# A conv block with an MLP on one core: where the sums of activations are staged, and after which products the gate columns come

## Chip, core, metric

One core of one Trainium2 chip. The metric is the device time of one execution in microseconds (us). The engines are TensorE (PE, with its weight loads PEld), VectorE (DVE), ScalarE (ACT), GpSimd (POOL) and SyncE (SP), whose queue issues nearly all DMAs, in order. Matmuls write to banks of PSUM, the other operands lie in SBUF.

## What is computed

One layer over 256 tokens of width 2048, in float32. For the kernel that is measured (`DEPTH` is 1) the mixer is the convolution.

```python
mod = silu(c) @ mod_w + mod_b                      # 2048 -> 6 x 2048
sh1, sc1, g1, sh2, sc2, g2 = split(mod, 6)
h = rms_norm(x, norm1_g) * (1 + sc1) + sh1
a, gt = split(h @ conv_w_in + conv_b_in, 2)
u = depthwise_conv(a * sigmoid(gt), width 31) + conv_dw_b
y = silu(layer_norm(u)) @ conv_w_out + conv_b_out
x = x + (1 + g1) * y
h = rms_norm(x, norm2_g) * (1 + sc2) + sh2
u = square(relu(h @ mlp_w1))                       # 2048 -> 8192
x = x + (1 + g2) * (u @ mlp_w2)                    # 8192 -> 2048
```

The change lies in the last two lines and in g2, the gate of the last one.

## The kernel before

**Precision by splitting.** Every float32 operand of a matmul is split into a rounded part `hi` (made by ACT, L228) and the remainder `lo` (a subtraction on DVE, L232; in earlier parts on POOL). A product is the sum of three matmuls, hi by hi, hi by lo, lo by hi. Weights arrive in tiles of 128 x 2048 (1024 KB) in a ring of seven `raw` buffers; each is split in two halves, into a ring of six `hi` and one of six `lo` buffers, 128 x 1024 each. ACT can fill a `hi` buffer only when its last reader is done.

**The MLP.** The hidden width is cut into four quarters. Of each quarter q come the "up" products (`mlp_w1`), then eight "down" products (`mlp_w2`), here called up 0, down 0, up 1 and so on. A down product i takes two weight tiles, so four halves, and issues 48 matmuls. Two down products fill one block of the output: even i starts it in a PSUM bank pair, odd i ends it (function `regions`; there are two such pairs, named `mm`). The order of the products is 0, 2, 1, 3, 4, 5, 6, 7. A finished block is emptied into the running output `y`, by ACT in down 0 (L1341), by an addition on DVE in down 1 and down 2 (L1343, "drain"), before its bank pair can be started again. In quarters 1 to 3 part of the up products is replaced by seven smaller ones, in the manner of Strassen ("seven"), four of which take sums and differences of the activations `hl` in place of `hl` itself.

**The sums.** These are the same for quarters 1 to 3. `make_sums(k2)` makes a quarter of them, four times in down 0: DVE adds hi and lo of two tiles (`a` and `b`, L353), takes four differences (`c` and `d`, L359), ACT rounds these (L363), DVE takes the remainder (L364), and eight DMAs write both to a DRAM buffer `kept` (L367), from which `load_sum` reads them at the start of each later up stage. `a`, `b`, `c`, `d` come from `two`, a ring of six buffers of 128 x 512 that many steps share. The rounded part and the remainder lie in a tile `st` from the ring of `hi` buffers. `SUMS_AT` lists the down products behind which a quarter of the sums is made.

**Gate columns.** The 16 tiles of g2 are each a product of a 128 x 2048 tile of `mod_w` with `silu(c)`, made by DVE as one long multiply with accumulation (L538, in `mod_col`) and a small addition (L493). Such a "column" takes one `raw` buffer and one load of 1024 KB. `LATE_GATE` tells after which up or down product how many of them are issued.

**Order.** A scheduler orders each engine's instructions from a priority, given by the place in the program, and its own time line. `urgent()` moves what stands in it ahead, as it does the splits of the next product's weights; `tc.issue_after(x)` keeps what stands in it behind instruction x on its engine. `state["w_lo"]` is the last weight remainder issued so far, `state["w_hi"]` the last rounding. DVE, ACT and SP carry out their instructions in that order.

Of the kernel before, what the change touches and what calls it, by code (L numbers as in the profile page):

```python
# [9 lines left out]
F32 = mybir.dt.float32  # L10
F32R = mybir.dt.float32r
AF = mybir.ActivationFunctionType
ALU = mybir.AluOpType
PSUM = bass.MemoryType.PSUM

P = 128
# [51 lines left out]
SPLIT_LOADS = [("col", SC1 * KT + KT - 1), ("col", SH1 * KT + KT - 1), ("first", KT - 1)]  # L68
POOLED = [("out", i) for i in range(6)] + [("up", 0, 1), ("up", 0, 2)]
IN_PSUM = range(1, 6)  # L70
LATE_GATE = {("up", 0): [0, 0, 0, 0, 1, 1, 1, 0], ("down", 0): [1, 1, 0, 0, 0, 0, 0, 0], ("down", 1): [0, 3, 0, 3, 3, 2, 0, 0]}
SEVEN = (1, 2, 3)
SUMS_AT = (2, 3, 4, 5)
SEVEN_JOBS = (1, 5, 7, (2,), 3, (3,), 6, (6,), 2, 4, (7,))
PLAIN = {"x": 4, "w": 0, "z": 1, "y": 5}
PLUS = {5: "w", 7: "z", 6: "z", 4: "y"}
# [3 lines left out]
def conv_block(ctx: ExitStack, tc: tile.TileContext, x, vec, dwq, c_row, mod_r, mod_t, mod_c, w_first, w_in, w_out, w1, w2, out):  # L80
    nc = tc.nc

    const = ctx.enter_context(tc.tile_pool(name="const", bufs=1))
    wts = ctx.enter_context(tc.tile_pool(name="wts", bufs=1))
# [38 lines left out]
    for i in range(2):  # L123
        p = ps.tile([P, 2, 2 * T], F32, name="mm", bufs=2)
# [6 lines left out]
    state = {"used": 0}  # L131
# [12 lines left out]
    def urgent():  # L144
        return tc.high_priority(offset=URGENT)

    HALF = KT // 2
# [202 lines left out]
    def make_sums(k2):  # L350
        a, b, c, d = [two() for _ in range(4)]
        for dst, src in ((a, hl[k2]), (b, hl[k2 + 4])):
            nc.vector.tensor_tensor(dst, src[:, :, 0:T].bitcast(F32), src[:, :, T : 2 * T].bitcast(F32), op=ALU.add)  # L353
        one, two_ = slice(0, P), slice(P, 2 * P)
        for dst, x0, x1 in (
            (c[:, :, one], a[:, :, two_], b[:, :, two_]), (d[:, :, one], a[:, :, one], c[:, :, one]),
            (c[:, :, two_], a[:, :, two_], a[:, :, one]), (d[:, :, two_], b[:, :, one], d[:, :, one]),
        ):
            nc.vector.tensor_tensor(dst, x0, x1, op=ALU.subtract)  # L359
        for ms, src in (((0, 2), c), ((1, 3), d)):  # L360
            st = wts.tile([P, HALF, P], F32R, name="hi", bufs=6).rearrange("p (h k m) n -> p h k m n", h=2, k=2)
            src = src.rearrange("p k (m n) -> p k m n", m=2)
            nc.scalar.activation(st[:, 0], src, AF.Copy)  # L363
            nc.vector.tensor_tensor(st[:, 1], src, st[:, 0].bitcast(F32), op=ALU.subtract)  # L364
            for j, m in enumerate(ms):
                for h in range(2):
                    nc.sync.dma_start(kept[m, :, 2 * k2 : 2 * k2 + 2, h, :], st[:, h, :, j, :].bitcast(F32))  # L367

    def load_sum(m):
        sums_of[m] = []  # L370
# [211 lines left out]
    def ps_two():  # L582
        return ps.tile([P, 2, T], F32, name="acc", bufs=2)

    def two():
        return tmp.tile([P, 2, T], F32, name="two", bufs=6)
# [6 lines left out]
    def spread(r):  # L593
        return r[:, None, :].to_broadcast([P, 2, T])
# [7 lines left out]
    def scaled(k2, r):  # L602
        n = two()
        nc.vector.tensor_tensor(n, pair_of(xs, k2), spread(r), op=ALU.mult)
        return n

    def modulate(k2, n, sh, sc, h):
        for c in range(2):
            k = 2 * k2 + c
            nc.scalar.activation(h[:, c, :], n[:, c, :], AF.Identity, scale=amps[sc][:, k : k + 1], bias=mcol(sh, k))  # L610
        split_act(new_hl(k2), h)
# [25 lines left out]
    for job in jobs:  # L637
        n = quota.get(job, 0)
# [3 lines left out]
        if job == ("in", KT - 2):  # L642
            after[job] = after[job] + scales
        if job[:2] in LATE_GATE:
            n = LATE_GATE[job[:2]][job[2]]
            after[job], last = last[:n], last[n:]
# [39 lines left out]
    def evac(p, cs=slice(0, 2), out=None):  # L686
        t1 = two()[:, cs, :]
        t2 = two()[:, cs, :] if out is None else out
        nc.scalar.activation(t1, p[:, cs, T : 2 * T], AF.Copy)
        nc.vector.tensor_tensor(t2, p[:, cs, 0:T], t1, op=ALU.add)  # L690
        return t2
# [3 lines left out]
    p = ps.tile([P, 512], F32, name="small", bufs=1)  # L695
    for k2 in range(HALF):
        s = two()
# [8 lines left out]
    with urgent():  # L706
        part = two()[:, 0, :]
        nc.scalar.activation(part, p[:, 0:T], AF.Copy)
        p = ps.tile([P, 512], F32, name="row", bufs=1)
# [8 lines left out]
    for _ in range(2):  # L718
        p = ps.tile([P, 2, 2 * T], F32, name="mm", bufs=2)
# [52 lines left out]
    for k in range(KT):  # L772
        c = k % 2
# [3 lines left out]
        if c == 0:  # L777
            n = two()
# [5 lines left out]
        h = h2[:, c, :]  # L784
# [121 lines left out]
    def fold_stats(sums):  # L906
        st = ps.tile([P, 2, 2 * T], F32, name="mm", bufs=2)
        for n in range(2):
            nc.tensor.matmul(st[:, n, 0:T], col("fold", n * P, P), sums, start=True, stop=False)
        return st  # L910
# [80 lines left out]
    def at_job(at, f, *args):  # L991
        tasks.setdefault(at, []).append(partial(f, *args))
# [40 lines left out]
    for n, job in enumerate(jobs):  # L1033
# [16 lines left out]
        kind, i = job[0], job[-1]  # L1050
# [14 lines left out]
        if kind == "out" and i > 0:  # L1065
            p = ps_two()
        elif not by_tokens(job):
            p = ps.tile([P, 2, 2 * T], F32, name="mm", bufs=2)
# [48 lines left out]
        if kind == "in":  # L1117
# [57 lines left out]
            with urgent(), tc.issue_after(state["row_end"].ins):  # L1175
                st = fold_stats(sums)
# [18 lines left out]
            with urgent():  # L1195
# [3 lines left out]
                ms = factor[:, T : 2 * T]  # L1199
# [4 lines left out]
            for k2 in range(HALF):  # L1204
# [17 lines left out]
                with urgent():  # L1222
                    nc.gpsimd.tensor_tensor(e, pair_of(cvs, k2), spread(mu), op=ALU.subtract)
                    state["e_end"] = nc.vector.tensor_tensor(e, e, spread(r), op=ALU.mult).ins
                    for c in range(2):
                        k = 2 * k2 + c
# [17 lines left out]
        if kind == "out":  # L1244
# [4 lines left out]
            with urgent():  # L1249
                for c in range(2):  # L1250
                    k = 2 * i + c
# [10 lines left out]
            a = two()  # L1262
            for c in range(2):
                k = 2 * i + c
# [27 lines left out]
        elif kind == "up":  # L1292
            if job[1:] == (0, 0):
                for k2 in range(HALF):
                    modulate(k2, scaled(k2, r2), SH2, SC2, ps_two())
            if plain:
                with urgent():
                    t2 = evac(p)
                    a = two()
                    nc.vector.tensor_tensor(t2, t2, spread(r2), op=ALU.mult)  # L1300
                    for c in range(2):
                        at = 2 * i + c
                        nc.scalar.activation(t2[:, c, :], t2[:, c, :], AF.Relu, bias=shc[:, at : at + 1])
                    nc.vector.tensor_tensor(a, t2, t2, op=ALU.mult)
                u2[i] = mp.tile([P, 2, 2 * T], F32R, name="u2", bufs=HALF)
                split_act(u2[i], a)
            elif i % 2 and job[1] in SEVEN:
                at_job(n + 1, block_out, n + 1, job[1], i // 2, sums.pop((kind, i // 2)))
            elif i % 2:
                with urgent():  # L1310
                    turn_block(job[1], i // 2, sums.pop((kind, i // 2)))
            mods(after[job])
            if job[1] == 0:
                if i == 0:
                    turned = scratch.tile([KT, P, T], F32, name="turned")
                    y = xs.rearrange("p k t -> p (k t)").rearrange("p (b f) -> p b f", b=2)
                turn(i)
        else:
            with tc.issue_after(state["w_lo"]):
                mods(after[job])  # L1320
            if job[1] == 0 and i in SUMS_AT:
                if i == SUMS_AT[0]:
                    kept = scratch.tile([4, P, HALF, 2, P], F32, name="kept")
                make_sums(SUMS_AT.index(i))
            if job == ("down", 1, 5):
                gates = scratch.tile([1, D], F32, name="gates")
                with tc.issue_after(state["load"].ins):
                    nc.sync.dma_start(gates[0].rearrange("(k p) -> p k", p=P), modc[:, G2 * KT : G2 * KT + KT])
            if job == ("down", 1, 7):
                with tc.issue_after(state["load"].ins):  # L1330
                    nc.sync.dma_start(cb, gates.to_broadcast([P, D]))
            if job[1] == 2 and i % 2 == 0:
                with tc.issue_after(state["load"].ins):
                    pieces[i // 2] = fetch(i // 2)
            if i % 2 == 0:
                continue
            for t, cs, p in sums.pop((kind, i // 2)):
                at = slice(512 * (i // 2) + cs.start, 512 * (i // 2) + cs.stop)
                s = y[:, t, at]
                if job[1] == 0:  # L1340
                    nc.scalar.activation(s, p, AF.Copy)  # L1341
                elif job[1] < QUARTERS - 1:
                    nc.vector.tensor_tensor(s, p, s, op=ALU.add)  # L1343
                    if job[1] == 2 and i < HALF - 1:
                        scale_y(s, at, pieces[i // 2][t])
                    elif job[1] == 2:
                        at_job(n + 4, scale_y, s, at, pieces[i // 2][t])
                else:
                    g = two().rearrange("p a t -> p (a t)")[:, cs]
                    with tc.issue_after(state["y_end"].ins) if "y_end" in state else ExitStack():  # L1350
                        nc.vector.tensor_tensor(g, p, cb[:, at], op=ALU.mult)
                    state["y_end"] = nc.vector.tensor_tensor(s, s, g, op=ALU.add)
                    nc.sync.dma_start(out[:, t, at], s)
# [60 lines left out]
```

## Time and profile before

| | |
|---|---|
| median of three runs | 1092.16 us (1090.88 to 1093.37) |
| the profiled execution | 1096.91 us, span 1095.1 us |
| PE busy | 1065.1 us, 97% of the span |
| DVE, ACT, POOL busy | 844.5, 582.2, 216.1 us |
| mean granted TensorE clock | 0.994 |
| DMA | 331.00 MB, 302 GB/s on average |

The profile is of one execution, which took 0.4% more than the median. A line such as L232 is the line of the kernel's source. `out<-in` names tiles; a releaser behind an arrow is what ended an idle time. PE is reported busy for nearly the whole span, and matmuls overlap, so a stage is better judged by how long its fixed number of matmuls takes.

### The profile page before, as it was taken

What the parts mean: (1) busy time and instruction counts of PE and PEld (TensorE: products, weight loads), DVE (VectorE), ACT (ScalarE), POOL (GpSimd) and SP (SyncE); (2) the same over time, 40 slices, a digit from 0 to 9 for tenths busy, and PEclk for the clock granted to TensorE, in tenths of its full rate; (3) what the DMA queues carried; (4) which work ended last, traced back from release to release, by engine and by line L of the source; (5) the groups of instructions that cost most, each with busy time, mean ns of one, the idle gap of its engine ahead of it and who ended that gap; (6) DMA issues with size and microseconds to landing.
All of it is one profiled execution on the core that took longest, in us unless ns stands there. A gap on an engine that the chain in (4) does not pass through costs nothing.

```text
span 1095.1 us, 15654 instructions
## 1 busy us (share of the span) xinstructions
PE 1065.1 (97%) x5928; PEld 880.1 (80%) x5928; DVE 844.5 (77%) x1105; ACT 582.2 (53%) x805; POOL 216.1 (20%) x147
## 2 busy tenths in 40 slices
PE   7999999999999999999999999699999999999998
PEld 4888876777799988887787888588888888788887
DVE  5777899988678878768478994888896678898563
ACT  4111398677875685444356475235565634556541
POOL 0000169989498270000000000000000000000000
PEclk9999999999999999999999999899999999999999
DMA  9999997997999868988775899985979983979921
GB/s 386 420 421 420 416 414 290 390 353 272 416 403 396 334 241 292 309 238 283 251 269 203 293 314 297 374 339 162 369 220 347 234 301 139 293 254 362 262 78 39
DMA packets 154478, 331.00 MB, mean 302 GB/s; under 512 B 88482, under 2 KB 114594, under 8 KB 119458
## 3 DMA queue, kind: packets, MB, share of 16 engines
q1 hardware_dynamic: 154256, 329.88, 83.3%
q8 instruction: 46, 0.75, 0.3%
q14 instruction: 30, 0.24, 0.1%
q10 hardware_dynamic: 146, 0.13, 0.0%
HBM read 313.71 MB, written 16.26 MB: 301 GB/s over the span
## 4 chain that ended last, share of the span: by engine, by line
PE 58%; DMA 19%; DVE 12%; SPq 4%; issue 3%; ACT 3%; DVEq 0%; ACTq 0%
DMA raw<-mod_c 10%; PE mm L297 9%; PE mm L298 9%; PE mm L299 9%; PE mm L260 6%; DVE lo L232 4%; DMA flat<-two 3%; SPq L404 3%; PE mm L261 3%; DVE raw L538 3%; PE acc L257 2%; PE acc L256 2%; PE acc L258 2%; DMA kept<-hi 2%; PE mm L950 2%
## 5 line engine op out<-in xcount | busy, mean ns | idle before, releaser
L228 ACT ACTIVATE hi<-raw 128x1024 fp32r<-128x1024 f32 x356 | 366.7, 1055 | 296.0 <-PE mm L299 180.6
L232 DVE TENSOR_TENSOR lo<-raw,hi 128x1024 fp32r<-128x1024 f32 x295 | 351.1, 1218 | 129.1 <-ACT hi L228 128.4
L297 PE MATMUL mm<-hi,u 128*128 128x512 f32 x496 | 194.5, 393 | 9.0 <-DVE x L1343 7.9
L298 PE MATMUL mm<-lo,u 128*128 128x512 f32 x496 | 194.8, 394 | 2.0 <-DVE lo L232 2.0
L299 PE MATMUL mm<-hi,u 128*128 128x512 f32 x496 | 194.1, 392 | 1.1 <-DVE u L246 1.1
L232 POOL TENSOR_TENSOR lo<-raw,hi 128x1024 fp32r<-128x1024 f32 x61 | 155.0, 2567 | 30.7 <-ACT hi L228 30.7
L538 DVE SCALAR_TENSOR_TENSOR raw<-raw,cond 128x2048 f32<-128x2048 f32 x50 | 116.0, 2332 | 30.8 <-DMA raw<-mod_c 30.8
L297 PEld LDWEIGHTS mm<-hi,u 128*128 128x128 f32 x496 | 94.1, 190 | 29.4 <-issue 8.2
L298 PEld LDWEIGHTS mm<-lo,u 128*128 128x128 f32 x496 | 94.2, 190 | 22.7 <-DVE lo L232 3.5
L299 PE MATMUL mm<-hi,hl 128*128 128x512 f32 x288 | 112.1, 389 | 0.0
L298 PE MATMUL mm<-lo,hl 128*128 128x512 f32 x288 | 112.0, 389 | 0.0
L297 PE MATMUL mm<-hi,hl 128*128 128x512 f32 x288 | 112.0, 389 | 0.0
L299 PEld LDWEIGHTS mm<-hi,u 128*128 128x128 f32 x496 | 94.2, 190 | 21.1 <-DVE u L246 1.5
L829 DVE SCALAR_TENSOR_TENSOR acc<-u,v,acc 128x256 f32<-128x256 f32 x230 | 91.5, 483 | 0.0
L260 PE MATMUL mm<-hl,hi 128*128 128x512 f32 x224 | 80.0, 401 | 0.0
L733 PE MATMUL mm<-two,first 128*128 128x256 f32 x240 | 57.5, 394 | 7.9 <-ACT two L791 7.9
L256 PE MATMUL acc<-hl,hi 128*128 128x256 f32 x224 | 63.4, 283 | 0.0
L257 PE MATMUL acc<-hl,hi 128*128 128x256 f32 x224 | 63.4, 283 | 0.0
L258 PE MATMUL acc<-hl,lo 128*128 128x256 f32 x224 | 63.4, 283 | 0.0
L298 PEld LDWEIGHTS mm<-lo,hl 128*128 128x128 f32 x288 | 54.1, 188 | 11.3
L297 PEld LDWEIGHTS mm<-hi,hl 128*128 128x128 f32 x288 | 54.1, 188 | 11.2
L299 PEld LDWEIGHTS mm<-hi,hl 128*128 128x128 f32 x288 | 54.1, 188 | 11.2
(265 smaller groups left out, 1681.2 us busy)
## 6 DMA issues: line engine op xcount, KB each, us to landing
raw<-w SPq DMA_DIRECT2D x128, 1024.0 KB, 7.3
raw<-mod_c SPq DMA_DIRECT2D x64, 1024.0 KB, 10.6
raw<-mod_r SPq DMA_DIRECT2D x28, 1024.0 KB, 8.5
raw<-w_in SPq DMA_DIRECT2D x16, 1024.0 KB, 10.5
raw<-w_out SPq DMA_DIRECT2D x16, 1024.0 KB, 8.6
first<-w_first SPq DMA_DIRECT2D x15, 1024.0 KB, 19.8
u<-kept SPq DMA_DIRECT2D x24, 512.0 KB, 7.6
flat<-two SPq DMA_DIRECT2D x30, 256.0 KB, 6.1
```

What stands on the lines that cost most here:

```text
L228: state["w_hi"] = nc.scalar.activation(hi, w[:, ks, :], AF.Copy).ins
L232: end = by.tensor_tensor(lo, w[:, ks, :], hi.bitcast(F32), op=ALU.subtract)
L256: nc.tensor.matmul(out_p, w, m[:, 0:T], start=begin, stop=False)
L257: nc.tensor.matmul(out_p, w, m[:, T : 2 * T], start=False, stop=False)
L258: state["mm_end"] = nc.tensor.matmul(out_p, lo[:, k % HALF, :], m[:, 0:T], start=False, stop=end)
L260: nc.tensor.matmul(p[:, c, :], hi[:, k % HALF, :], m, start=(k == 0), stop=(k == KT - 1))
L297: nc.tensor.matmul(p, p_hi, hi, start=begin, stop=False)
L298: nc.tensor.matmul(p, p_hi, lo, start=False, stop=False)
L299: nc.tensor.matmul(p, p_lo, hi, start=False, stop=end)
L538: end = nc.vector.scalar_tensor_tensor(w, w, 1.0, cb, op0=ALU.mult, op1=ALU.mult, accum_out=acc)
L733: step = nc.tensor.matmul(held[n][:, c, :], w[:, 2 * n + c, :], h, start=k == 0 and c == 0, stop=k == KT - 1, skip_group_check=True)
L829: end = nc.vector.scalar_tensor_tensor(out, s, w, acc, op0=ALU.mult, op1=ALU.add)
```

## The change

Three things change. The tiles `st` are gone: the rounded parts go into `a` and `b`, which are no longer needed then, and the remainders into `c` and `d` in place; the DMAs write from there. The sums are made behind products 2, 1, 3, 4 instead of 2, 3, 4, 5, and kept behind the last weight split. The gate columns are spread anew over the products, and kept behind the last drain on DVE that was issued before them.

```diff
-LATE_GATE = {("up", 0): [0, 0, 0, 0, 1, 1, 1, 0], ("down", 0): [1, 1, 0, 0, 0, 0, 0, 0], ("down", 1): [0, 3, 0, 3, 3, 2, 0, 0]}
+LATE_GATE = {("up", 0): [0, 0, 0, 1, 1, 1, 1, 0], ("down", 0): [1, 0, 0, 0, 0, 1, 1, 0], ("down", 1): [0, 2, 0, 2, 2, 3, 0, 0]}
-SUMS_AT = (2, 3, 4, 5)
+SUMS_AT = (2, 1, 3, 4)
...
-        for ms, src in (((0, 2), c), ((1, 3), d)):
-            st = wts.tile([P, HALF, P], F32R, name="hi", bufs=6).rearrange("p (h k m) n -> p h k m n", h=2, k=2)
-            src = src.rearrange("p k (m n) -> p k m n", m=2)
-            nc.scalar.activation(st[:, 0], src, AF.Copy)
-            nc.vector.tensor_tensor(st[:, 1], src, st[:, 0].bitcast(F32), op=ALU.subtract)
+        for ms, src, hi in (((0, 2), c, a), ((1, 3), d, b)):
+            nc.scalar.activation(hi.bitcast(F32R), src, AF.Copy)
+            nc.vector.tensor_tensor(src.bitcast(F32R), src, hi, op=ALU.subtract)
             for j, m in enumerate(ms):
-                for h in range(2):
-                    nc.sync.dma_start(kept[m, :, 2 * k2 : 2 * k2 + 2, h, :], st[:, h, :, j, :].bitcast(F32))
+                for h, part in enumerate((hi, src)):
+                    nc.sync.dma_start(kept[m, :, 2 * k2 : 2 * k2 + 2, h, :], part[:, :, P * j : P * j + P])
...
-            with tc.issue_after(state["w_lo"]):
+            with tc.issue_after(state["w_lo"]), tc.issue_after(state.get("drain", state["w_lo"])):
                 mods(after[job])
...
-                make_sums(SUMS_AT.index(i))
+                with tc.issue_after(state["w_lo"]):
+                    make_sums(SUMS_AT.index(i))
...
-                    nc.vector.tensor_tensor(s, p, s, op=ALU.add)
+                    state["drain"] = nc.vector.tensor_tensor(s, p, s, op=ALU.add).ins
```

From L360 on the changed kernel's lines are one or two lower: L364 is L362 there, L538 is L536, L1343 is L1342. PE's order is the same in both, and POOL's.

On DVE, in down 0, before, the second of the four sums and the start of the third. L353 to L364 are the sum, L232 the remainder of a weight half.

```order
L353 TENSOR_TENSOR two<-hl 128x512 x2
L232 TENSOR_TENSOR lo<-raw,hi 128x1024
L359 TENSOR_TENSOR two<-two 128x2x128
L364 TENSOR_TENSOR hi<-two,hi 128x512
L359 TENSOR_TENSOR two<-two 128x2x128
L364 TENSOR_TENSOR hi<-two,hi 128x512
L359 TENSOR_TENSOR two<-two 128x2x128
L353 TENSOR_TENSOR two<-hl 128x512 x2
L359 TENSOR_TENSOR two<-two 128x2x128 x3
L232 TENSOR_TENSOR lo<-raw,hi 128x1024
```

On DVE at the same place now, the first sum and the start of the second:

```order
L353 TENSOR_TENSOR two<-hl 128x512 x2
L359 TENSOR_TENSOR two<-two 128x2x128 x2
L232 TENSOR_TENSOR lo<-raw,hi 128x1024
L359 TENSOR_TENSOR two<-two 128x2x128 x2
L232 TENSOR_TENSOR lo<-raw,hi 128x1024
L362 TENSOR_TENSOR two<-two 128x512 x2
L232 TENSOR_TENSOR lo<-raw,hi 128x1024 x2
L353 TENSOR_TENSOR two<-hl 128x512 x2
L359 TENSOR_TENSOR two<-two 128x2x128 x2
```

Before, parts of successive sums ran into each other; now each sum is spread over the four weight halves of one product, and the next begins behind them.

On ACT, in down 0, before: L228 rounds a weight half, L363 the sums, L1341 empties a block, L243 rounds a hidden activation.

```order
L243 ACTIVATE u_4640<-two 128x2x256
L228 ACTIVATE hi<-raw 128x1024
L363 ACTIVATE hi<-two 128x512 x2
L228 ACTIVATE hi<-raw 128x1024 x6
L1341 ACTIVATE x_2504<-mm 128x512 x2
L228 ACTIVATE hi<-raw 128x1024 x2
```

On ACT at the same place now:

```order
L243 ACTIVATE u_4640<-two 128x2x256
L243 ACTIVATE u_4644<-two 128x2x256
L228 ACTIVATE hi<-raw 128x1024 x4
L361 ACTIVATE two<-two 128x512 x2
L228 ACTIVATE hi<-raw 128x1024 x4
L1340 ACTIVATE x_2504<-mm 128x512 x2
```

The roundings of a sum no longer write into the ring of `hi` buffers, and stand behind four weight halves each.

On DVE, in down 1, before, from the splits of the last two hidden activations (u_6093, u_6098, L246) to the additions that empty the first two blocks (L1343); L538 is a gate column, L493 its small addition.

```order
L246 TENSOR_TENSOR u_6093<-two,u_6093 128x2x256
L232 TENSOR_TENSOR lo<-raw,hi 128x1024
L538 SCALAR_TENSOR_TENSOR raw,modc<-raw,cond 128x2048 x3
L246 TENSOR_TENSOR u_6098<-two,u_6098 128x2x256
L232 TENSOR_TENSOR lo<-raw,hi 128x1024
L493 TENSOR_TENSOR modc<-modc,v 128x1 x2
L232 TENSOR_TENSOR lo<-raw,hi 128x1024 x2
L493 TENSOR_TENSOR modc<-modc,v 128x1
L232 TENSOR_TENSOR lo<-raw,hi 128x1024
L538 SCALAR_TENSOR_TENSOR raw,modc<-raw,cond 128x2048 x3
L1343 TENSOR_TENSOR x_2504<-mm,x_2504 128x512 x2
```

On DVE at the same place now:

```order
L246 TENSOR_TENSOR u_6093<-two,u_6093 128x2x256
L232 TENSOR_TENSOR lo<-raw,hi 128x1024
L536 SCALAR_TENSOR_TENSOR raw,modc<-raw,cond 128x2048 x2
L246 TENSOR_TENSOR u_6098<-two,u_6098 128x2x256
L232 TENSOR_TENSOR lo<-raw,hi 128x1024
L491 TENSOR_TENSOR modc<-modc,v 128x1 x2
L232 TENSOR_TENSOR lo<-raw,hi 128x1024 x3
L1342 TENSOR_TENSOR x_2504<-mm,x_2504 128x512 x2
L536 SCALAR_TENSOR_TENSOR raw,modc<-raw,cond 128x2048 x2
L232 TENSOR_TENSOR lo<-raw,hi 128x1024
L1342 TENSOR_TENSOR x_2504<-mm,x_2504 128x512 x2
```

Two columns instead of three stand ahead of the split of u_6098, and the next ones have moved from ahead of the first additions to behind them.

## The prediction

> **What bounds the kernel now.** I read the times first, then the page's share of engines, then the busy time by stage, and only then single rows. TensorE (PE) is busy nearly everywhere, so what can be won is where it is not. The MLP alternates "up" products (the first matrix) and "down" products (the second) by quarter of the hidden width. The view of windows, cut at the edges of those stages, has per row: the stretch and its length, busy time of PE, weight loads, DVE, ACT and POOL, the granted clock, the DMA share and GB/s.
>
> ```profile
> span 1095.1 us, 15654 instructions
> 474.60:567.90 93.30, 90.13 (x386) 72.86 (x385) 64.55 (x81) 40.84 (x50) 0.00 (x0) 0.98 0.84 280
> 567.90:651.90 84.00, 82.21 (x362) 67.43 (x361) 74.80 (x66) 53.59 (x61) 0.00 (x0) 1.00 0.71 243
> 651.90:751.10 99.20, 90.26 (x385) 73.83 (x384) 75.67 (x82) 40.12 (x44) 0.00 (x0) 0.95 0.90 320
> 751.10:833.10 82.00, 81.92 (x361) 67.51 (x360) 73.90 (x68) 51.99 (x58) 0.00 (x0) 1.00 0.82 282
> 833.10:920.20 87.10, 87.10 (x386) 72.12 (x385) 57.48 (x60) 40.11 (x44) 0.00 (x0) 1.00 0.86 270
> ```
>
> These are down 0, up 1, down 1, up 2 and down 2. The three down stages issue the same 384 matmuls (the view adds one or two at the edges). Down 2 takes 87.10 us with PE busy throughout, so 10.89 us for each of its eight products is the price without a stall. Against it down 0 loses 6.2 us and down 1 loses 12.1. Up 1 loses 2.0 against up 2, which does the same work. Together 20.3 us: the change touches nothing else that waits, and this is its ceiling.
>
> Where they are lost, from PE's timeline (start, duration, idle before and releaser):
>
> ```profile
> 511.16 0.50 PE L298 MATMUL mm<-lo,u 128*128 128x512 f32 x1 [0.76 <-DVE lo L232]
> 545.68 0.50 PE L297 MATMUL mm<-hi,u 128*128 128x512 f32 x1 [1.19 <-ACT hi L228]
> 546.94 0.79 PE L298 MATMUL mm<-lo,u 128*128 128x512 f32 x1 [0.76 <-DVE lo L232]
> 549.66 0.61 PE L298 MATMUL mm<-lo,u 128*128 128x512 f32 x1
> 550.09 0.42 PE L299 MATMUL mm<-hi,u 128*128 128x512 f32 x1
> 581.23 0.50 PE L347 MATMUL acc<-lo,u 128*128 128x512 f32 x1 [1.66 <-DVE lo L232]
> 692.09 0.50 PE L299 MATMUL mm<-hi,u 128*128 128x512 f32 x1 [1.09 <-DVE u L246]
> 696.53 0.39 PE L299 MATMUL mm<-hi,u 128*128 128x512 f32 x1
> 704.77 0.76 PE L297 MATMUL mm<-hi,u 128*128 128x512 f32 x1 [7.86 <-DVE x L1343]
> 705.34 0.63 PE L298 MATMUL mm<-lo,u 128*128 128x512 f32 x1
> 705.76 0.63 PE L299 MATMUL mm<-hi,u 128*128 128x512 f32 x1
> ```
>
> In down 0 PE waits for split weights, in down 1 above all for the addition of L1343, which empties a bank. Each longer wait is paid twice: behind it a matmul starts every 0.43 us (549.66 to 550.09, 705.34 to 705.76) instead of every 0.227 (87.10 by 384).
>
> **Sums through the `two` buffers.** ACT's timeline shows why the weights are late in down 0:
>
> ```profile
> 508.78 4.86 ACT L228 ACTIVATE hi<-raw 128x1024 fp32r<-128x1024 f32 x5 [8.36 <-DMA kept<-hi]
> 531.12 2.95 ACT L228 ACTIVATE hi<-raw 128x1024 fp32r<-128x1024 f32 x3 [7.90 <-DMA kept<-hi]
> 544.57 2.95 ACT L228 ACTIVATE hi<-raw 128x1024 fp32r<-128x1024 f32 x3 [8.50 <-DMA kept<-hi]
> 557.44 6.75 ACT L228 ACTIVATE hi<-raw 128x1024 fp32r<-128x1024 f32 x7 [6.97 <-DMA kept<-hi]
> ```
>
> Four sums each put two staging tiles into the ring of six `hi` buffers, so ACT's next split waits 7 to 8.5 us until the writes to `kept` have landed: 31.7 us of ACT, of which PE feels 6.2 and, through a DVE that enters up 1 late, the 1.66 at 581.23. The change takes these tiles away. Its work stays: per sum two additions from `hl`, four half-size differences, two roundings on ACT, two remainders and eight writes, with the same shapes. Nothing is saved in busy time, only the four waits. But the wait does not vanish. `two` has six buffers and a sum now uses four until its writes land; so the next sum finds two free for its additions, and its differences wait for the writes of the first two. That wait sits on DVE, and queued behind it are the `lo` splits that PE needs, and the roundings on ACT with the `hi` splits behind them. What it costs I work out from these rows:
>
> ```profile
> 474.62 0.39 PE L297 MATMUL mm<-hi,u 128*128 128x512 f32 x1
> 492.68 0.69 DVE L416 SCALAR_TENSOR_TENSOR two<-two 128x512 f32<-128x512 f32 x1 [0.53 <-DMA two<-flat]
> 481.96 1.27 DVE L353 TENSOR_TENSOR two<-hl 128x512 f32<-128x512 f32 x2
> 522.37 0.76 DVE L359 TENSOR_TENSOR two<-two 128x256 f32<-128x256 f32 x2
> 535.63 1.29 DVE L364 TENSOR_TENSOR hi<-two,hi 128x512 fp32r<-128x512 f32 x2
> 479.09 2.31 DVE L232 TENSOR_TENSOR lo<-raw,hi 128x1024 fp32r<-128x1024 f32 x2
> 522.18 7.58 SPq L367 DMA_DIRECT2D kept<-hi  x8
> L367 SPq DMA_DIRECT2D kept<-hi x32: 359/486/1437, 495.5 to 553.0; - x32
> DMA to landing us min/median/max: 3.0/6.6/8.6
> ```
>
> The first sum now starts behind the last square (492.68, released by a transfer, which the change does not move), one split, two splits of `u` (0.6 each) and two more: 493.4 + 1.1 + 1.2 + 2.3 = 498.0. It takes 1.2 for the additions, 0.7 and 0.7 for the differences, a split behind each (1.1), 1.2 for the remainders: 504.0. The writes start when the first remainder is done, 0.6 earlier, behind one weight load on SP's queue (0.35). By the medians the last one that counts is issued 7 x 0.49 later and lands 6.6 later: 9.8 after the sum's end. The next sum then needs the second pair of differences, a split and the remainders, 3.0. So a sum takes 12.8 us where a product takes 10.9, and DVE falls back 1.9 us a sum: ends at 504.0, 516.8, 529.6, 542.4. The last sum holds the splits of product 6, which PE wants at 474.62 + 6 x 10.89 = 540.0 and, the second, 2.7 later. They are done 4.0 and 1.2 before 542.4, at 538.4 and 541.2: 1.6 and 1.5 us to spare. Before, ACT and DVE were already late at 511.16. So I expect the waits of down 0 to go nearly whole and leave 0.7 for jitter: 6.2 - 0.7 = 5.5.
>
> Bounds: with landings at the minimum, 3.0, a sum takes 9.2 and nothing is left (6.2). At the maximum, 8.6, it takes 14.8; the last sum ends at 548.4 and its second split 4.5 us late, 6 with the half clock: nothing is won. I take the median because the eight writes follow 1024 KB weight loads now as then.
>
> In up 1 the DVE then starts earlier. Two columns have moved into products 5 and 6 (2.2 each) and eat part of it, so I count 1.4 of the 2.0.
>
> The sums at products 2, 1, 3, 4 instead of 2, 3, 4, 5 issue no more. The last writes land by 542.4 + 9.8 = 552, and the first product that reads `kept` is the second of up 1, some 5 us after 474.6 + 87.1 = 561.7: nothing waits for them. On SP's queue the writes stand ahead of weight loads, which wait for DVE's splits to empty a `raw` buffer; seven of these, three and a half products of weights, cover that.
>
> **Gate columns.** DVE's timeline in down 1:
>
> ```profile
> 684.72 2.28 DVE L538 SCALAR_TENSOR_TENSOR raw<-raw,cond 128x2048 f32<-128x2048 f32 x1
> 691.35 0.69 DVE L246 TENSOR_TENSOR u<-two,u 128x512 fp32r<-128x512 f32 x1
> 691.95 1.22 DVE L232 TENSOR_TENSOR lo<-raw,hi 128x1024 fp32r<-128x1024 f32 x1
> 696.71 2.29 DVE L538 SCALAR_TENSOR_TENSOR raw<-raw,cond 128x2048 f32<-128x2048 f32 x1
> 703.34 1.29 DVE L1343 TENSOR_TENSOR x<-mm,x 128x512 f32<-128x512 f32 x2
> ```
>
> Three columns (684.72 to 691.35, 2.21 each with their accumulator read) precede the last split of `u`; three more (696.71 to 703.34) precede the additions. Now two stand in front of that split: it starts at 684.72 + 4.42 = 689.1 and ends at 689.7, where PE issued its last matmul before the wait at 690.62 (692.09 less 1.09 idle and the 0.38 of the matmul before). Then four weight splits (4 x 1.14) and small additions (0.2) end at 694.5, and now come the additions of L1343, 0.60 each: first half of the bank at 695.1, second at 695.7. PE ends its fourth product at 651.9 + 4 x 10.89 = 695.4 and wants the second half three matmuls (0.7) later. So the two waits (1.36 and 10.8 with the half clock) go, with 0.3 us to spare; I leave 0.5. The columns follow the additions, two by two, 4.4 beside 4.6 of splits and 1.3 of additions in 10.9: they fit, product 5's three too (6.6 + 4.6 = 11.2, additions 1.2, by a DVE which then is over 5 us ahead). Gain 12.1 - 0.5 = 11.6, between 12.1 and 9 (a lateness of one column's half, 1.1, and its half clock, 2).
>
> The loads move with the columns: sixteen of 1024 KB as before, two less in down 1. In down 0 and in up 0 one more each. Of up 0:
>
> ```profile
> 411.07 1.21 DVE L232 TENSOR_TENSOR lo<-raw,hi 128x1024 fp32r<-128x1024 f32 x1
> 427.82 2.29 DVE L538 SCALAR_TENSOR_TENSOR raw<-raw,cond 128x2048 f32<-128x2048 f32 x1 [1.67 <-DMA raw<-mod_c]
> ```
>
> The new column stands ahead of the split at 411.07, whose product starts at 474.62 - 5 x 10.89 = 420.2: 8 us of cover against 2.2 plus a load's wait like the 1.67 here. Cost nothing; without the cover 4.
>
> **Sum.** 5.5 + 1.4 + 11.6 = 18.5 us of a span of 1095.1, whose execution took 1096.91. The median of three runs is 1092.16, 0.4% less, and the gain scales to 18.4: 1073.7.
>
> **Rivals.** First, the wait only changes engine: landings near 8.6 keep down 0 and up 1 as they are and only down 1 gains: 1092.2 - 11.6 = 1080.6. For it speaks that the 7 to 8.5 us waits on ACT are the same transfers; against it the median. A rule of the Trainium skill (TensorE: Matmul & The Clock Gate, "Why this matters for your kernels") bears on its price: gaps under about 3 us should not lower the clock. The row of 546.94 disagrees, 1.19 and 0.76 idle were enough; by the rule the stall would cost 4.5 instead of 6 and the time be 1079.1.
>
> Second, DVE reaches the additions of down 1 late after all, since only 0.3 us are spare: one column's 2.2 plus its half clock of about 3 remains, 1073.7 + 5 = 1078.7.
>
> Third, slower: the loop of the sums on DVE turns into the bound of down 0. With the issue of 522.18 (7.58 by 8, 0.95 each) and 8.6 to land, a sum takes 18.0, the last ends at 558 and splits come 14 us late, with three half clocks of 3 us 23 us. Against the 8.2 lost now and 11.6 won in down 1 the time is 1092.2 + 14.8 - 11.6 = 1095.4. It decides from a period of 16.9, that is 14 us from a sum's end to its last landing. Nothing in the rows comes near for four sums in a row.
>
> **Numbers.** Forecast 0.62, for itself 1071 to 1077; wait on DVE 0.18; late additions 0.14; slower 0.04; the remaining 0.02 is no difference. The range 1070.8 to 1081.5 runs from the ceiling (1092.2 - 20.3 = 1071.9, and a microsecond of jitter) past the first two rivals. 0.2% of this kernel, 2.2 us, is about what a measurement can tell. Faster 0.94, same 0.02, slower 0.04.
>
> **What would show it.** Down 0 and down 1 at 87 to 88.5 us, up 1 under 83; no ACT wait on `kept`; three DVE waits on `kept` of 2 to 5 us at the differences; no PE wait on the additions over 0.5, clock 1.00. Wrong if a down stage stays over 91, or if PE waits on `lo` at the start of products 4 to 6.

## The result, and the profile after

| | before | after |
|---|---|---|
| median of the timed runs | 1091.52 us (1090.88 to 1093.37, 4 runs) | 1076.21 us (1075.71 to 1077.26, 4 runs) |
| profiled execution | 1096.91, span 1095.1 | 1075.87, span 1074.1 |
| PE busy | 1065.1 us, 97% | 1058.6 us, 99% |
| TensorE clock | 0.994 | 1.000 |

The ratio is 0.9858 (95% interval 0.9841 to 0.9875): 15.3 us or 1.4% faster. The forecast was 1073.7, with a range of 1070.8 to 1081.5. Between the two profiled executions the gain is 21.0 us; why the medians show less is the main question of the experiments.

The view of windows of the changed kernel, cut at the edges of down 0, up 1, down 1, up 2 and down 2; the columns are those of the prediction's first table:

```profile
span 1074.1 us, 15646 instructions
474.30:561.30 87.00, 87.00 (x385) 72.06 (x384) 70.76 (x87) 42.45 (x51) 0.00 (x0) 1.00 0.93 306
561.30:643.20 81.90, 81.90 (x361) 67.49 (x361) 72.92 (x66) 52.73 (x60) 0.00 (x0) 1.00 0.76 261
643.20:730.40 87.20, 87.20 (x385) 72.00 (x385) 69.83 (x75) 40.27 (x44) 0.00 (x0) 1.00 0.95 342
730.40:812.40 82.00, 81.92 (x361) 67.49 (x360) 74.30 (x69) 52.05 (x58) 0.00 (x0) 1.00 0.85 280
812.40:899.50 87.10, 87.10 (x386) 72.11 (x385) 57.19 (x59) 40.11 (x44) 0.00 (x0) 1.00 0.87 267
```

The second number of a row is the length, the third PE's busy time: they agree in each of the first three stages. Those three last 256.1 us where they lasted 276.5 (87.0 + 81.9 + 87.2 against 93.3 + 84.0 + 99.2), and now equal down 2 and up 2. The whole ceiling of 20.3 us is taken, and the clock is 1.00 in all five. Windows are cut to a tenth of a microsecond; a stage length with two decimals in the text runs from a stage's first matmul to the first of the next.

No wait of ACT on `kept` is left. What came in its place is in the view of waits (total, times, longest) and in DVE's timeline:

```profile
DVE two L359 <- DMA kept<-two: 9.5, 3, 3.8
513.00 0.89 DVE L359 TENSOR_TENSOR two<-two 128x256 f32<-128x256 f32 x2 [2.81 <-DMA kept<-two]
523.52 0.76 DVE L359 TENSOR_TENSOR two<-two 128x256 f32<-128x256 f32 x2 [3.83 <-DMA kept<-two]
534.93 0.76 DVE L359 TENSOR_TENSOR two<-two 128x256 f32<-128x256 f32 x2 [2.90 <-DMA kept<-two]
```

Three waits at the differences, as forecast, 9.5 us together instead of ACT's 31.7, and PE feels none. In down 1, lines of DVE's timeline from the second column to the one behind the first block's additions:

```profile
677.85 2.29 DVE L536 SCALAR_TENSOR_TENSOR raw<-raw,cond 128x2048 f32<-128x2048 f32 x1
680.06 0.69 DVE L246 TENSOR_TENSOR u<-two,u 128x512 fp32r<-128x512 f32 x1
681.94 3.49 DVE L232 TENSOR_TENSOR lo<-raw,hi 128x1024 fp32r<-128x1024 f32 x3
685.35 1.28 DVE L1342 TENSOR_TENSOR x<-mm,x 128x512 f32<-128x512 f32 x2
686.54 2.29 DVE L536 SCALAR_TENSOR_TENSOR raw<-raw,cond 128x2048 f32<-128x2048 f32 x1
```

The additions (L1342) end at 686.6 and the next column comes behind them. PE ends its fourth product at 643.2 + 4 x 10.89 = 686.8, so the bank is free in time, by 0.2 us.

### The profile page after: what moved, and what is told of

The parts are those of the page before. It is cut to its first block, busy times and chain, and to the rows that moved or that the text cites. A ratio compares the mean times of both kernels' runs of the same rounds, so it can differ in the third digit from the quotient of the medians.

```text
span 1074.1 us, 15646 instructions
## 1 busy us (share of the span) xinstructions
PE 1058.6 (99%) x5928; PEld 877.6 (82%) x5928; DVE 847.2 (79%) x1105; ACT 582.1 (54%) x805; POOL 216.5 (20%) x147
## 4 chain that ended last, share of the span: by engine, by line
PE 84%; DMA 8%; DVE 5%; ACT 1%; issue 1%; SPq 0%; DVEq 0%; ACTq 0%
PE mm L298 16%; PE mm L299 16%; PE mm L297 16%; DMA raw<-mod_c 7%; PE mm L260 6%; PE mm L261 3%; PE acc L256 3%; PE acc L257 3%; PE acc L258 3%; PE mm L948 2%; PE row L444 2%; PE acc L347 2%; PE acc L348 2%; PE acc L346 1%; DVE raw L536 1%; DVE lo L232 1%
## 5 line engine op out<-in xcount | busy, mean ns | idle before, releaser
L228 ACT ACTIVATE hi<-raw 128x1024 fp32r<-128x1024 f32 x356 | 366.9, 1055 | 250.2 <-PE mm L299 177.2
L232 DVE TENSOR_TENSOR lo<-raw,hi 128x1024 fp32r<-128x1024 f32 x295 | 351.2, 1219 | 97.5 <-ACT hi L228 96.9
L298 PE MATMUL mm<-lo,u 128*128 128x512 f32 x496 | 192.5, 389 | 0.0
L232 POOL TENSOR_TENSOR lo<-raw,hi 128x1024 fp32r<-128x1024 f32 x61 | 155.4, 2574 | 32.0 <-ACT hi L228 32.0
L536 DVE SCALAR_TENSOR_TENSOR raw<-raw,cond 128x2048 f32<-128x2048 f32 x50 | 117.5, 2359 | 30.3 <-DMA raw<-mod_c 30.3
L297 PEld LDWEIGHTS mm<-hi,hl 128*128 128x128 f32 x288 | 54.1, 188 | 11.3
```

The costliest lines, as they stand in the source:

```text
L228: state["w_hi"] = nc.scalar.activation(hi, w[:, ks, :], AF.Copy).ins
L232: end = by.tensor_tensor(lo, w[:, ks, :], hi.bitcast(F32), op=ALU.subtract)
L297: nc.tensor.matmul(p, p_hi, hi, start=begin, stop=False)
L298: nc.tensor.matmul(p, p_hi, lo, start=False, stop=False)
L536: end = nc.vector.scalar_tensor_tensor(w, w, 1.0, cb, op0=ALU.mult, op1=ALU.mult, accum_out=acc)
```

## Experiments

Two theories for the 5.7 us between 21.0 and 15.3: the typical execution of the kernel before loses less in down 0 and up 1 than the profiled one (called D0 in the expectations), or less in down 1 (D1).

**The gate columns alone** (new table, its entry for up 0 included, and the wait for the drain; sums as before):

```diff
-LATE_GATE = {... ("down", 0): [1, 1, 0, 0, 0, 0, 0, 0], ("down", 1): [0, 3, 0, 3, 3, 2, 0, 0]}
+LATE_GATE = {... ("down", 0): [1, 0, 0, 0, 0, 1, 1, 0], ("down", 1): [0, 2, 0, 2, 2, 3, 0, 0]}
-            with tc.issue_after(state["w_lo"]):
+            with tc.issue_after(state["w_lo"]), tc.issue_after(state.get("drain", state["w_lo"])):
```

> Only the gate columns are moved and kept behind the drains; the sums are staged and placed as before. The forecast's theory: the two halves of the change are independent. Down 1 comes to 87 to 88.5 us (99.20 before), down 0 stays at 92 to 94 and up 1 at 84 to 86, so a profiled execution gains 11 to 12 us on 1095.1. What the timed runs gain is the open question: the whole change gained 15.3 us by medians and 21.0 between the profiled executions. Theory D0 (the typical execution loses less than the profiled one in down 0 and up 1): this kernel gains the full 11.6 to 12, time 1079.5 to 1080. Theory D1 (it loses less in down 1): this kernel gains only about 7, time 1084 to 1085.

Measured: 1083.52 us, ratio 0.9922 (0.9909 to 0.9936). Windows of down 0, up 1 and down 1, and PE's waits in up 1:

```profile
474.40:562.60 88.20, 87.44 (x386) 72.04 (x385) 65.22 (x84) 42.67 (x51) 0.00 (x0) 1.00 0.87 287
562.60:650.30 87.70, 82.78 (x362) 67.21 (x361) 79.40 (x69) 53.67 (x61) 0.00 (x0) 1.00 0.75 261
650.30:737.90 87.60, 87.34 (x386) 72.01 (x385) 69.94 (x75) 40.24 (x44) 0.00 (x0) 1.00 0.95 340
571.69 0.50 PE L347 MATMUL row<-lo,u 128*128 128x512 f32 x1 [1.60 <-DVE lo L232]
576.34 0.50 PE L346 MATMUL acc<-hi,u 128*128 128x512 f32 x1 [1.61 <-ACT hi L228]
579.66 0.50 PE L347 MATMUL acc<-lo,u 128*128 128x512 f32 x1 [1.67 <-DVE lo L232]
```

The time is near D1's number, but not for D1's reason: down 1 gains what was forecast (99.2 to 87.6). Instead up 1 is 3.8 us longer than before, so the edits are not independent. With the sums as before, three waits of 1.6 us stand in up 1 where the prediction's rows had one. Down 0 is at 88.2, where I had expected 92 to 94.

**The sums alone** (staging and places changed, old table, no wait for the drain):

> Only the sums are changed (staged in the buffers of their terms, behind products 2, 1, 3, 4); the gate columns stand as before. The forecast's theory: down 0 at 87 to 88.5 us (93.30 before), up 1 at 82 to 83 (84.00), down 1 still at 97 to 100 with a wait of 6 to 8 us on the addition that empties the bank; a profiled execution gains 7 to 8 us. Timed: D0 says a gain of only about 3 us (1088 to 1089), D1 a gain of about 8 (1083 to 1084). Rival: the sums' earlier end also brings DVE earlier into down 1 and takes part of that wait, then down 1 is under 95 and the two halves overlap.

Measured: 1088.20 us, ratio 0.9961 (0.9949 to 0.9973). Windows of the three stages, and PE's two waits:

```profile
474.50:561.50 87.00, 87.00 (x385) 72.04 (x384) 66.86 (x81) 42.02 (x48) 0.00 (x0) 1.00 0.90 298
561.50:643.40 81.90, 81.90 (x362) 67.50 (x361) 71.78 (x65) 52.68 (x60) 0.00 (x0) 1.00 0.71 242
643.40:743.10 99.70, 90.37 (x386) 73.91 (x385) 75.70 (x82) 40.22 (x44) 0.00 (x0) 0.95 0.90 319
684.02 0.50 PE L299 MATMUL mm<-hi,u 128*128 128x512 f32 x1 [1.50 <-DVE u L246]
696.71 0.77 PE L297 MATMUL mm<-hi,u 128*128 128x512 f32 x1 [7.84 <-DVE x L1342]
```

Down 0 and up 1 are without a stall, down 1 as before: DVE's earlier start does not reach it. The timed gain is 4.1 us, as D0 says, though against the first profile the two stages are 8.4 us shorter.

**The kernel before, profiled again, twice.**

> The kernel before once more, unchanged, for a second profile of it. If its stalls vary from execution to execution, this profile has a span of 1089 to 1092 us and one of the stages down 0 (93.30 in the first profile), up 1 (84.00) or down 1 (99.20) is 4 to 5 us shorter: D0 says down 0 and up 1 (together 172 to 173 instead of 177.3), D1 says down 1 (94 to 95). If instead the profile itself makes stalls longer, the span is near 1095 again while the timed runs stay at 1091.

> The kernel before, unchanged, for a third profile. In the first, two waits of 1.19 and 0.76 us in down 0 were followed by 3 us at the half clock (down 0 93.26), in the second waits of 0.64 and 0.76 were not (90.00). My theory: the half clock behind short waits is the exception and the first profile an execution at the slow end: span 1088 to 1092, no half clock in down 0, about 5 us of it in down 1 as both times. Rival: waits of about 2 us together lower the clock each time they occur: where the two waits at the start of a product sum to 1.9 or more, a half clock of 3 us stands behind them.

Measured: spans 1091.0 and 1090.3; as the same kernel against itself the ratio was 1.000 (0.9988 to 1.0011). Windows of down 0, up 1 and down 1 of the second profile and its wait of ACT on `kept`, then the windows of the third:

```profile
475.00:565.00 90.00, 87.95 (x386) 71.92 (x385) 62.95 (x79) 39.84 (x48) 0.00 (x0) 1.00 0.84 282
565.00:648.90 83.90, 82.13 (x361) 67.38 (x360) 75.43 (x67) 53.48 (x61) 0.00 (x0) 1.00 0.72 246
648.90:747.40 98.50, 89.98 (x385) 73.64 (x384) 75.02 (x82) 40.11 (x44) 0.00 (x0) 0.95 0.90 320
ACT hi L228 <- DMA kept<-hi: 26.0, 4, 8.3
```

```profile
474.50:563.50 89.00, 87.73 (x386) 71.95 (x385) 61.96 (x78) 40.03 (x48) 0.00 (x0) 1.00 0.83 280
563.50:647.40 83.90, 82.16 (x361) 67.39 (x360) 75.55 (x67) 53.54 (x61) 0.00 (x0) 1.00 0.72 245
647.40:746.80 99.40, 90.12 (x385) 73.73 (x384) 75.01 (x81) 40.12 (x44) 0.00 (x0) 0.95 0.90 318
```

Up 1 and down 1 repeat within 1 us; down 0 was 93.3, then 90.0, then 89.0. That is D0: of the 4.1 and 4.8 us by which these two executions were shorter than the first (1092.84 and 1092.11 against 1096.91), 3.3 and 4.3 lie in down 0. The first profile was of an unusually long execution: the 35 further timed runs of the kernel before that ran beside these experiments lie between 1089.51 and 1096.16, and it took 1096.91. What it shows that the others do not is a stretch at half the clock in down 0 (0.98 in its window, 1.00 here) and longer waits of ACT on `kept`, 31.7 us against 26.0 in the second profile.

**Without the wait for the drain:**

```diff
-            with tc.issue_after(state["w_lo"]), tc.issue_after(state.get("drain", state["w_lo"])):
+            with tc.issue_after(state["w_lo"]):
```

> The whole change but for one line: the gate columns stand at their new places without being kept behind the last drain, so that in down 1 two columns precede the first additions again, as three did before. My theory: DVE is behind PE at that point, so the additions come 4.4 us later than in the changed kernel, at about 699 to 700 where PE wants the bank at 695.4 (in the time of the first profile of before); PE waits about 4 us and then runs 2 to 3 us at the half clock: down 1 at 91 to 94 us, time 1080 to 1083. Rival: with one column less ahead of the last split of u, DVE has caught up and the drain line is worth nothing: 1076 to 1077.

Measured: 1083.80 us, ratio 0.9918 (0.9905 to 0.9932), so 7.6 us slower than the changed kernel by the times and 6.6 by the ratios, which take each run against the kernel before that ran beside it. Down 1's window, DVE's additions, PE's wait and the clock behind it:

```profile
643.50:738.50 95.00, 90.14 (x385) 74.00 (x384) 70.38 (x75) 40.23 (x44) 0.00 (x0) 0.96 0.92 317
690.56 1.29 DVE L1342 TENSOR_TENSOR x<-mm,x 128x512 f32<-128x512 f32 x2
692.00 0.77 PE L297 MATMUL mm<-hi,u 128*128 128x512 f32 x1 [4.86 <-DVE x L1342]
695.00:700.00 5.00, 5.00 (x17) 3.86 (x17) 1.68 (x3) 1.06 (x1) 0.00 (x0) 0.69 0.94 347
```

The mechanism held, the size was beyond the expectation: the wait is 4.86 us and the half clock behind it adds 95.0 - 87.0 - 4.9 = 3.1. The line carries over half of what the columns' part gains.

**The old table with the wait for the drain:**

> The whole change but for the table: the gate columns stand behind their old products (down 1: 0, 3, 0, 3, 3, 2), but are kept behind the last drain on DVE. My theory: the drain line is what removes the long wait in down 1, the table only the short one. Three columns still precede the last split of u, so PE waits about 1 to 1.5 us there and runs some 3 us at the half clock; the wait of 7.8 on the addition is gone or under 1: down 1 at 88.5 to 91 us, time 1077.5 to 1080. Rival: without one column less ahead of that split DVE is behind at the addition too, by 2 us or more: down 1 at 92 to 95, time 1081 to 1084.

Measured: 1080.53 us, ratio 0.9875 (0.9856 to 0.9895). Down 1's window and PE's waits:

```profile
643.60:734.70 91.10, 87.82 (x387) 72.12 (x386) 73.72 (x82) 39.90 (x44) 0.00 (x0) 1.00 0.98 361
684.77 0.50 PE L299 MATMUL mm<-hi,u 128*128 128x512 f32 x1 [2.07 <-DVE u L246]
690.81 0.47 PE L297 MATMUL mm<-hi,u 128*128 128x512 f32 x1 [1.21 <-DVE x L1342]
```

Between theory and rival: the long wait shrinks to 1.21, the short one grows to 2.07, and the clock stays at 1.00. Both edits of the columns' part are needed.

**The staging undone** (sums at the new places, in the `hi` ring again), profiled twice:

```diff
-        for ms, src, hi in (((0, 2), c, a), ((1, 3), d, b)):
-            nc.scalar.activation(hi.bitcast(F32R), src, AF.Copy)
+        for ms, src in (((0, 2), c), ((1, 3), d)):
+            st = wts.tile([P, HALF, P], F32R, name="hi", bufs=6).rearrange("p (h k m) n -> p h k m n", h=2, k=2)
...
```

> The whole change but for the staging: the sums stand behind products 2, 1, 3, 4 and the gate columns at their new places, but the rounded parts and remainders go into two tiles of the ring of hi buffers again. My theory: the staging carries what the sums' part gains. ACT waits four times for the writes to kept, 5 to 8.5 us each, and PE feels some of it: down 0 at 88 to 92 us, up 1 at 83 to 86 (87.04 and 81.90 in the changed kernel), time 1079.5 to 1084. Rival: being one product sooner is enough, the waits fall where ACT is ahead: 1076 to 1077, with the ACT waits in the trace and no PE wait behind them.

> The kernel with the sums staged in the hi ring at the new places, for a second profile: in the first, waits of 1.31 and 0.76 us in down 0 left the clock at 1.00, though they are longer together than the 1.19 and 0.76 that lowered it in the kernel before. My theory: the clock stays at 1.00 in down 0 again, down 0 at 90 to 92.5. Rival: whether the clock falls is chance from one execution to the next, and it falls here: PE clock at 0.6 to 0.7 in one stretch of 5 us and down 0 at 93 to 95.

Measured: 1081.25 us, ratio 0.9880 (0.9862 to 0.9899). ACT's wait, the windows of down 0 and up 1, PE's two waits that stand closest, and the clock around them:

```profile
ACT hi L228 <- DMA kept<-hi: 15.8, 5, 5.2
474.70:566.50 91.80, 88.29 (x386) 71.76 (x385) 70.33 (x86) 42.97 (x51) 0.00 (x0) 1.00 0.83 290
566.50:648.70 82.20, 81.89 (x362) 67.51 (x361) 73.90 (x66) 52.56 (x60) 0.00 (x0) 1.00 0.75 259
533.39 0.50 PE L297 MATMUL mm<-hi,u 128*128 128x512 f32 x1 [1.31 <-ACT hi L228]
534.65 0.50 PE L298 MATMUL mm<-lo,u 128*128 128x512 f32 x1 [0.76 <-DVE lo L232]
530.00:540.00 10.00, 7.93 (x34) 6.00 (x33) 6.56 (x10) 3.83 (x5) 0.00 (x0) 1.00 0.56 195
```

With the sums sooner ACT's waits are shorter (15.8 us against 31.7 and 26.0 before), and still PE loses 4.8 us in down 0, in the second profile 4.3 (91.34). The staging is what frees down 0; the places by themselves do not. In both profiles the clock stayed at 1.00.

**The places undone** (staging in `two`, sums behind products 2, 3, 4, 5):

> The whole change but for the places of the sums, which stand behind products 2, 3, 4, 5 again; staged in the buffers of their terms, gate columns at their new places. My theory: the last sum falls together with the gate columns behind products 5 and 6, ends at about 552 instead of 540, and DVE enters up 1 late: down 0 at 87 to 88, up 1 at 84 to 86, no ACT wait on kept; time 1078 to 1081. Rival: the places are worth nothing once the ring of hi is left free: 1076 to 1077, up 1 under 82.5.

Measured: 1077.35 us, ratio 0.9847 (0.9831 to 0.9863); down 0 87.0, up 1 81.9, down 1 87.9. My expectation missed: up 1 does not move at all, although the last sum ends near 550 instead of 540. DVE's waits on `kept` fall to 0.5 us in all. Up 1's window, and the wait that explains most of the 0.7 us by which down 1 is longer:

```profile
561.30:643.20 81.90, 81.90 (x362) 67.50 (x361) 72.45 (x65) 52.66 (x60) 0.00 (x0) 1.00 0.74 252
687.51 0.47 PE L297 MATMUL mm<-hi,u 128*128 128x512 f32 x1 [0.64 <-DVE x L1342]
```

The places are worth nothing that these runs can tell.

**Five buffers in `two`:**

```diff
-        return tmp.tile([P, 2, T], F32, name="two", bufs=6)
+        return tmp.tile([P, 2, T], F32, name="two", bufs=5)
```

> The changed kernel with five buffers in the ring two instead of six, which shifts a few instructions ahead of 474 us as well, so it is read by stages. A sum now finds only one free buffer instead of two, and its second addition waits for the writes of the sum before. The loop model of the prediction: what DVE now does ahead of its wait (an addition, two differences, a split, about 3 us) comes behind it, the period of a sum grows from 11.7 to 14 to 15 us, the last sum ends at about 548 and the second split of product 6 is 3 to 5 us late: down 0 at 90 to 94 us. Rival: DVE has slack that the model does not see, the waits grow to 5 to 6 us each and stay covered: down 0 at 87.0 to 87.5.

Measured: 1076.20 us, ratio 0.9837 (0.9822 to 0.9853). DVE's waits and the window of down 0:

```profile
DVE two L353 <- DMA kept<-two: 7.1, 2, 3.7
DVE two L359 <- DMA kept<-two: 5.2, 2, 4.8
474.20:561.20 87.00, 87.00 (x385) 72.09 (x384) 69.96 (x87) 42.66 (x51) 0.00 (x0) 1.00 0.90 295
```

The rival was right that the waits stay covered: they grow from 9.5 to 12.3 us, the last sum ends at 541.8, and nothing is late. It had put them at 5 to 6 us each; none is over 4.8.

**Where the 3.8 us of up 1 came from**: the first kernel of this section with the old columns in up 0 and down 0, and 0, 2, 0, 3, 3, 3 in down 1.

> The kernel before with the drain line, and a table that differs in down 1 alone (0, 2, 0, 3, 3, 3 instead of 0, 3, 0, 3, 3, 2); up 0, down 0 and the sums as before. It asks where the 3.8 us come from by which up 1 was longer with the new table alone (87.74 against 83.98). My theory: they come from the two columns behind products 5 and 6 of down 0, where the sums as before still hold ACT and DVE. Without them up 1 is back at 83.5 to 84.5 us, down 0 at 89 to 94, down 1 at 87 to 88: time 1079 to 1081.5, under the 1083.5 of the new table alone. Rival: the columns of down 0 have no part in it, up 1 is at 86 to 88 again and the time at 1082 to 1085.

Measured: 1081.38 us, ratio 0.9900 (0.9884 to 0.9916); down 0 88.6, up 1 84.0, down 1 87.9, up 2 83.65. Up 1's window:

```profile
562.90:646.90 84.00, 82.22 (x361) 67.43 (x360) 75.42 (x66) 53.56 (x61) 0.00 (x0) 1.00 0.73 246
```

Up 1 is back, so it was the columns moved into up 0 and to the end of down 0, beside sums that still held ACT and DVE. Only the pair was changed, not each alone. Up 2 is 1.65 us longer, by a wait of that length on DVE's split. The old table with the wait for the drain has one of 1.20 near the same place, so it comes with eleven columns in down 1 kept behind the drains, and not only with the one moved to the end; the two were not tested apart.

**A version with more margin**: one column less ahead of the first additions (0, 1, 0, 2, 3, 3 in down 1).

> The changed kernel with one column moved within down 1: behind its products 0, 1, 0, 2, 3, 3 instead of 0, 2, 0, 2, 2, 3. One column of 2.2 us less stands ahead of the first additions that empty a bank. In the three profiles with the drain line PE waited 0.07, 0.43 and 0.64 us there, so that place has no margin. My theory: the wait goes to zero in every execution, down 1 at 87.04 to 87.1 us, and the median falls by 0 to 1 us, to 1075.3 to 1076.3. Rival: three columns behind the fifth product make DVE late at the next additions or at the splits of the seventh product: a PE wait of 0.5 us or more there, down 1 over 87.5, time 1076.5 to 1078.

Measured: 1076.39 us, ratio 0.9857 (0.9842 to 0.9873). The wait on the additions is gone, but a wait of 0.43 us on ACT appears in up 2 (82.5 us instead of 82.0). Nothing is won, and none of these versions measurably beats the changed kernel.

## Why the prediction was right, and which term was off

**Mechanisms.** Both held. The staging tiles in the `hi` ring caused the waits of down 0 (4.3 to 4.8 us come back with them), and the columns ahead of the additions those of down 1. All signs named for the changed kernel appeared, stage lengths, three DVE waits of 2.8 to 3.8 us and the clock among them.

**The terms of the sum.** Against the same profiled execution:

| stage | lost before | forecast gain | measured gain |
|---|---|---|---|
| down 0 | 6.2 | 5.5 | 6.2 |
| up 1 | 2.0 | 1.4 | 2.1 |
| down 1 | 12.1 | 11.6 | 12.0 |

The leftovers of 0.7, 0.6 and 0.5 us were not needed in this profile. The 0.5 in down 1 was well placed all the same: the changed kernel's profile shows no wait there, but with the same columns PE waited 0.64 us with the places undone, 0.43 with five buffers and 0.64 in the second profile of the staging undone, so the 0.3 us to spare are about none.

**The step that failed** is the last: "the gain scales to 18.4". The execution that was summed took 4.75 us more than the median, and I spread that over the whole span as a factor. Most of it was stall, and it lay in the very term that the change removes: down 0 lost 6.2 us in that execution, 3.0 and 1.9 in the next two. The 4.75 had to come off the gain. Off the 20.3 us that were there to win it leaves 15.6 and a time of 1076.6, where 1076.21 was measured; off my own sum of 18.5 it would have left 13.75 and 1078.4. So two errors worked against each other: the leftovers made the gain 1.8 us too small, the scaling made it over 4 us too large, and that the forecast of 1073.7 missed by only 2.5 us is in part luck. The row that hinted at it was in the first table: down 0's clock of 0.98.

**The period of the sums.** Forecast 12.8 us, measured 11.3, 12.3 and 11.4. From a sum's end to the release of the waiting difference pass 8.1, 7.3 and 6.4 us; I had 9.8. Behind the release, to the end of the next sum, come 3.2, 5.0 and 5.0 us where I had 3.0: in the last two sums it is the first pair of differences that waits, and not the second. The two errors partly cancel in the period. With five buffers the last sum ends at 541.8, about where I had put it for six (542.4), and nothing is late, as the 1.5 us to spare had it. What my expectation of that run got wrong is the growth of the period, from 11.7 to 12.6 us on average instead of 14 to 15.

**Independence.** I added the parts. Alone they gain 0.39 and 0.78%, together 1.42%. The prediction saw that two columns had moved into down 0 but weighed them against a DVE already set free. Without the staging they make up 1 3.8 us longer.

**The rivals.** That the wait only changes engine fell: it does, but under cover. Late additions are what comes without the drain line, at 1083.8 us rather than 1078.7: two columns stand ahead there, not one, and the wait is 4.86 us. The sums' loop as the bound did not come near even with five buffers.

**The clock rule.** The prediction set one row (1.19 and 0.76 us idle, then half the clock) against the Trainium skill (TensorE: Matmul & The Clock Gate, "Why this matters for your kernels"), by which PE should have no idle gap over about 3 us; I read it as saying that shorter gaps leave the clock alone. The runs speak mostly for that reading: waits of 1.31 and 0.76, of 1.60 to 1.67 and of 2.07 us left it at 1.00, behind waits of 4.86 us and more it was halved each time. The first profile's row stays an exception without an explanation. The prediction also let the rule spare a stall of 4.5 us; in one gap that is more than 3 us, and the wait of 4.86 us here was not spared.

## What to carry to other kernels

When the profiled execution is slower than the median, look for where the surplus lies before scaling: if it sits in a stall that the change removes, it comes off the gain. A ring whose buffers feed the bound engine should not also hold data that wait for a slow write; a ring of scratch on an engine with slack can, and the wait is then hidden. Keep filler work behind the instruction that frees the bound engine's bank, by an explicit order: here that one line was worth about 7 us.

## What the hardware showed that I had not expected

A wait of PE has two prices. Waits of 4.86 us and over cost their own length and about 3 us more, at the half clock (3.1 without the drain line; 99.7 - 87.0 - 1.5 - 7.8 = 3.4 with the sums alone). Waits of up to 2.07 us cost a few tenths beside their length (91.1 - 87.0 - 3.3 = 0.8 for two), except once: in the first profile of before, the half clock came behind waits of 1.19 and 0.76 us, and in another kernel it did not behind 1.31 and 0.76. What decides it was not settled. The same program's down 0 varied by 4.3 us over three profiles (93.3, 90.0, 89.0), while its up 1 stayed within 0.1.
